# Hybrid decoder trunk: the second norm's statistics for half the tokens amid the next output tile, and one weight chunk less loaded at the head of the feed-forward's loop along k

## The chip, the cores and the metric

The kernel runs on 1 core of a Trainium2 chip (trn2). The metric is the device time of one execution in microseconds (us). The kernel before took 1461.12 us (median of 3 runs, 1460.99 to 1461.18).

The engines are named as in the profile: PE (matmul) and PEld (its weight load), DVE (VectorE), ACT (ScalarE), POOL (GpSimd) and SP, which issues most of the loads.

## The reference, cut to what matters

Two layers (DEPTH = 2) act on x, 512 tokens by 1024 features, float32:

```python
h = rmsnorm(x, norm1_w) * (1 + sc1) + sh1
u = h @ w_in                       # pool, conv, attention and gate inputs
...
x = x + g1 * (merged @ w_out)
h2 = rmsnorm(x, norm2_w) * (1 + sc2) + sh2
x = x + g2 * ((jax.nn.silu(h2 @ w_gate) * (h2 @ w_up)) @ w_down)
```

The change touches the seam between `x + g1 * (merged @ w_out)`, the second rmsnorm, and the first products `h2 @ w_gate` and `h2 @ w_up`. The rmsnorm needs, for each token, the mean of the squares of all 1024 features of the new x, so it can't be finished for a token before every output tile of that token is done.

## The kernel before, in words

**Layout.** x lies transposed in SBUF: eight tiles x0 to x7 of 128 features by 512 tokens. A product is made as three matmuls of rounded float32 parts (`mm3`, L159): high by high, high by low, low by high. So every operand, weight or activation, has a high and a low half: ACT writes the high one by a copy into the rounded type, DVE writes the low one as the difference.

**Weights.** They come in chunks of up to eight 128x128 blocks in the order in which they are used. `load_w` (L334) takes the next chunk: SP issues its load into one of three raw buffers, and `split_w` (L325) makes its two halves, `whi` on ACT and `wlo` on DVE, into one of five buffers each. A raw buffer comes free when both halves are written. `next_w(ahead)` (L351) hands out the oldest loaded chunk and first loads until more than `ahead` chunks are there, so `ahead` are left behind it; without an argument it takes `ahead_now`, which is 4 here. The `wlo` differences are pinned: DVE runs them where the program has them. While `hold[0]` is set (L329), they are also placed behind the instruction it names.

**The output product.** `tail` (L961) makes the eight output tiles n = 0 to 7 of `merged @ w_out`. Tiles 0 to 5 are made for all 512 tokens. The last two (`halved=2`) are made by halves of 256 tokens: n = 6 and 7 for the first half, then n = 6 and 7 for the second. A half tile has 8 steps along k of three matmuls, 24 matmuls. After each tile `residual` (L958, DVE) adds it into x, and `nrm.add` squares the new x and adds it to a running sum (L460 on ACT, L461 on DVE; for tile 7 the product L463 on DVE, kept apart).

**The norm.** `stat` (L465) sums the squares over the features with two matmuls against a matrix of ones, in plain float32, and `newton` (L470) makes the reciprocal root: L474 on ACT, then L475, L476 and L477 on DVE. `apply` (L481) makes one tile of h2 for a range of tokens: L485 on DVE scales, L487 on ACT gives the high half, L488 on DVE the low half, L491 on ACT a plain float32 copy for the later forms.

**The order at the seam.** When the second half of tile 6 is done, `lead()` (called at L984) takes the statistics of the first 256 tokens and applies them to h2 tiles k = 0, 1, 2, while PE makes the second half of tile 7. In the lead, `hold[0]` is set to the last L488. The feed-forward then begins with a loop along k (`HALVES + REST`, L1108): steps n = 0, 1, 2 are k = 0, 1, 2 for the first 256 tokens, steps 3, 4, 5 the same k for the other 256, then k = 3 to 7 for all 512. Each step feeds six products, three gate and three up columns, all open in PSUM until k = 7. At step n = 1, ahead of its matmuls, `second` (L521) lifts the hold, takes the statistics of the other 256 tokens and applies them to everything that is left. The weights of step k are one chunk of 384 KB, taken at the first step that uses it (L1114). For k of 4 and more `make_forms` (L1030) derives combinations of h2 tiles for a later stage. After the loop come one gate and one up column by themselves, then pairs of columns that use the forms.

**Who sets the order.** PE's order is the program's. A planner orders the other engines by its own costs, apart from the pinned instructions. Every engine works off its instructions in order.

The first norm of layer 1 passes through `tail` too, with four halved tiles (`halved=4`) and its own lead.

Of the kernel before, what the change touches and what calls it, by code (L numbers as in the profile page):

```python
# [25 lines left out]
KT = D // P  # L26
# [53 lines left out]
def hybrid_trunk(ctx, tc, xT, ws, ada, cols, pool_w, qk_w, crow, pos, con, out):  # L80
# [22 lines left out]
    def ps_mm():  # L103
        return psum.tile([P, S], F32, tag="mm", name=nm("mm"), bufs=4)

    def ps_pair():
        return psum.tile([P, 2, S], F32, tag="pair", name=nm("pair"), bufs=2)
# [23 lines left out]
    def flush_bulk():  # L131
        while bulk:
            bulk.popleft()[1]()

    def tick():
        for f in list(fibers):
            f[0] -= 1
            if f[0] <= 0:
                n = next(f[1], None)
                if n is None:  # L140
                    fibers.remove(f)
                else:
                    f[0] = n
        run_bulk(bulk_rate[0])

    def drain():
        while fibers:
            tick()

    def matmul(*a, **k):  # L150
        tc.keep_in_program_order(T.matmul(*a, **k))  # L151
# [7 lines left out]
    def mm3(o, lhs, rhs, start, stop, main=True, **more):  # L159
        matmul(o, lhs[0], rhs[0], start=start, stop=False, **more)  # L160
        matmul(o, lhs[0], rhs[1], start=False, stop=False, **more)
        matmul(o, lhs[1], rhs[0], start=False, stop=stop, **more)
        if main:
            clock[0] += o.shape[-1]
            if clock[0] >= TICK:
                clock[0] -= TICK
                tick()

    def cut(pair, *ix):
        return pair[0][ix], pair[1][ix]  # L170

    def table(func, after):

        A.activation(sm([P, 1], tag="tab", bufs=1), after, func)
# [159 lines left out]
    def load_w():  # L334
        while at[1] < min(at[0] + 1 + SUMS_AHEAD, len(items)):
            sums, sub = items[at[1]]
            if sums is not None and sub == 0:
                sums.begin()
            at[1] += 1
        sums, what = items[at[0]]  # L340
        at[0] += 1
        if sums is not None:
            return sums.load(what)
        l, blocks = what
        raw = rawt()
        fetch(raw, l, blocks)
        return split_w(raw, len(blocks))
# [3 lines left out]
    def next_w(ahead=None):  # L351
        ahead = ahead_now[0] if ahead is None else ahead
        while at[0] < len(items) and len(loaded) <= ahead:
            loaded.append(load_w())
        return loaded.popleft()

    def wblk(w, b):
        return w[0][:, b, :], w[1][:, b, :]
# [54 lines left out]
    def ada_tasks(l, parts, early=False):  # L413
        out = []
        for part in parts:
            for j in range(KT):
                out.append((1.2, lambda part=part, j=j: ada_step(l, part, j, early)))
            out.append((0.2, lambda part=part: ada_end(l, part)))
        return out
# [101 lines left out]
    def second(nrm, l, i, bank):  # L521

        hold[0] = None
        nrm.stat(BLOCK, S, bank)
        for k, lo, hi in HALVES[3:] + REST:
            nrm.apply(l, i, k, lo, hi)
# [193 lines left out]
    for l in range(L):  # L720
# [6 lines left out]
        held = {}  # L727
        for n, (k, lo, hi) in enumerate([(k, 0, S) for k in range(KT)] if l == 0 else HALVES + REST):
# [18 lines left out]
            h = norm.k(k)  # L747
# [13 lines left out]
        def feature_tile(o, w):  # L761
            for k in range(KT):
                mm3(o, wblk(w, k), norm.k(k), k == 0, k == KT - 1)
# [193 lines left out]
        def residual(k, src, lo, hi, part):  # L957
            V.scalar_tensor_tensor(x[k][:, lo:hi], src, mod[l][:, part, k:k + 1], x[k][:, lo:hi],  # L958
                                   op0=ALU.mult, op1=ALU.add)

        def tail(src_of, wblk_of, part, nk, nrm, last, lead=None, halved=2):  # L961

            for n in range(KT - halved):
                if n == KT - halved - 1:
                    flush_bulk()
                o = ps_mm()
                for k in range(nk):
                    mm3(o, wblk_of(n, k), src_of(k), k == 0, k == nk - 1)
                residual(n, o, 0, S, part)
                if nrm is not None:  # L970
                    nrm.add(n, 0, S)
                if last:
                    nc.sync.dma_start(out[n * P:(n + 1) * P, :], x[n])
            for h in range(2):
                c = slice(h * BLOCK, (h + 1) * BLOCK)
                for n in range(KT - halved, KT):
                    o = ps_mm()
                    for k in range(nk):
                        mm3(o[:, :BLOCK], wblk_of(n, k), cut(src_of(k), slice(None), c), k == 0, k == nk - 1)
                    residual(n, o[:, :BLOCK], h * BLOCK, (h + 1) * BLOCK, part)  # L980
                    if nrm is not None:
                        nrm.add(n, h * BLOCK, (h + 1) * BLOCK)
                        if h == 1 and n == KT - halved:
                            lead()  # L984
                    if last:
                        nc.sync.dma_start(out[n * P:(n + 1) * P, c], x[n][:, c])
# [12 lines left out]
        def lead(nrm, ll, i, bank):  # L999

            def go():
                nrm.stat(0, BLOCK, bank)
                for k, lo, hi in HALVES[:3]:
                    hold[0] = nrm.apply(ll, i, k, lo, hi)
            return go
# [14 lines left out]
        def glu(g, u):  # L1020
            t = tmp()
            A.activation(t, g, AF.Silu)
            V.tensor_mul(t, u, t)
            act.append(split_from(t))
# [79 lines left out]
        for part, (along, single, pairs) in enumerate(PARTS):  # L1104
            act = []
            nk = along + single + 2 * pairs
            if along:
                held = {}  # L1108
                for n, (k, lo, hi) in enumerate(HALVES + REST):
                    if n == 1:  # L1110
                        second(norm, l, 1, bank)
                        table(AF.Silu, norm.y[:, 0:1])
                    if k not in held:
                        held[k] = next_w()  # L1114
                    for z in range(2 * FA):
                        mm3(f_ps[z][:, lo:hi], wblk(held[k], z), cut(norm.k(k), slice(None), slice(lo, hi)),
                            k == 0 and lo == 0, k == KT - 1)
                    if k >= HK:
                        make_forms(k - HK)
                del held  # L1120
                for z in range(FA):
                    glu(f_ps[z], f_ps[FA + z])
            for _ in range(single):
                wg = next_w()
                g = ps_mm()
                feature_tile(g, wg)
                u = ps_mm()
                feature_tile(u, next_w())
                glu(g, u)
            bulk_rate[0] = 0.0  # L1130
            for p in range(pairs):
                glu_pair(p == pairs - 1)
            if l + 1 < L:
                if part == 0:
                    later = ada_tasks(l + 1, (SC1, SH1, SC2, SH2))
                n = DOTS[part]
                bulk.extend(later[:n])
                del later[:n]
            bulk_rate[0] = 1.5
            blk = Blocks(nk, 4)  # L1140
            if part + 1 < len(PARTS):
                for n in range(KT):
                    if n == KT // 2:
                        bulk_rate[0] = 0.0
                    o = ps_mm()
                    for k in range(nk):
                        mm3(o, blk(n, k), act[k], k == 0, k == nk - 1)
                    residual(n, o, 0, S, G2)
            elif l + 1 == L:
                tail(lambda k: act[k], blk, G2, nk, None, True)  # L1150
            else:
                flush_bulk()
                drain()
                bulk.extend(later[:5])
                del later[:5]
                bulk_rate[0], credit[0] = 0.8, 0.0
                n1 = Norm()
                table(AF.Abs_reciprocal_sqrt, f32(act[-1][1])[:, 0:1])
                scratch = ps_pair()
                bank = scratch[:, 1]  # L1160
                tail(lambda k: act[k], blk, G2, nk, n1, False, lead(n1, l + 1, 0, bank), 4)
                norm = n1
# [100 lines left out]
```

## Time and profile before

| what | value |
|---|---|
| median of 3 runs | 1461.12 us (1460.99 to 1461.18) |
| profiled execution, its own time | 1461.3 us |
| its span in the profile | 1459.5 us |
| PE busy | 1451.3 us, 99% |
| DVE busy | 1053.5 us, 72% |
| ACT busy | 665.8 us, 46% |
| POOL busy | 105.9 us, 7% |
| PE on the chain that ended last | 96% |
| matmuls | 8443 |

The timeline lists instructions in order of time: start in us from the start of the span, duration in us (of a run of equal instructions, from the first start to the last end), engine, line, operation, output and input, shapes, and the count. What stands in brackets is idle time of that engine just before and what ended it. The ends of matmuls are modelled and overlap the next start, so the distance between two starts tells what PE lost better than its idle time does. Layer 0 passes the seam at 381 to 397 us, layer 1 at 1100 to 1117 us.

### The profile page before, as it was taken

Reading aid. Unit: us, or ns where it says so; the run is one execution under the profiler, and the core shown is the slowest. Engines: PE = TensorE matmul, PEld = TensorE weight load, DVE = VectorE, ACT = ScalarE, POOL = GpSimd, SP = SyncE. Lnnn points to the kernel's source line nnn. Section 1 sums busy time; section 2 is a strip of 40 time slices with the busy share of each in tenths; the row PEclk is TensorE's granted clock in tenths of the full one; section 3 lists DMA queues with packets and bytes.
Section 4 is the critical chain, followed back from the end, with each engine's and each line's share of the span. In section 5 each row is a group of like instructions: output and inputs, shape, how many; then the busy total and the mean of one; then the engine's idle time right before and its main releaser. Section 6 shows DMA issues by size and latency. Waiting matters only on the chain.

```text
span 1459.5 us, 21946 instructions
## 1 busy us (share of the span) xinstructions
PE 1451.3 (99%) x8443; PEld 1267.9 (87%) x8443; DVE 1053.5 (72%) x1855; ACT 665.8 (46%) x1138; POOL 105.9 (7%) x157
## 2 busy tenths in 40 slices
PE   9999999999999999999999999999999999999998
PEld 7888888788989998989988878788889889989997
DVE  7988888748686867677797766776587757657663
ACT  4634555443454452535444355555335525534450
POOL 0000000001100210211000000000020102111200
PEclk9999999999999999999999999999999999999999
DMA  9645334445336766756545422222462436637522
GB/s 351 219 142 173 121 110 138 137 159 152 109 114 205 201 174 202 188 146 203 191 146 176 161 77 73 73 77 98 158 194 78 138 122 165 183 98 192 137 85 84
DMA packets 84409, 217.19 MB, mean 149 GB/s; under 512 B 10832, under 2 KB 23760, under 8 KB 84304
## 3 DMA queue, kind: packets, MB, share of 16 engines
q1 hardware_dynamic: 67456, 177.37, 35.9%
q0 software_dynamic: 16128, 37.76, 11.8%
q8 instruction: 66, 1.08, 0.3%
q10 hardware_dynamic: 720, 0.66, 0.1%
q14 instruction: 39, 0.32, 0.1%
HBM read 213.65 MB, written 2.10 MB: 148 GB/s over the span
## 4 chain that ended last, share of the span: by engine, by line
PE 96%; DVE 2%; DMA 1%; ACT 1%; issue 0%; SPq 0%; ACTq 0%
PE mm L151 82%; PE pair L151 13%; PE mm L157 2%; DVE wlo L330 1%; DMA w<-in_ada 0%; DMA x<-in_xT 0%; DVE w L376 0%; ACT whi L327 0%; DVE tmp L485 0%; DVE big L504 0%; DVE big L488 0%; ACT big L487 0%; ACT big L491 0%; DVE tmp L476 0%; DVE big L477 0%
## 5 line engine op out<-in xcount | busy, mean ns | idle before, releaser
L151 PE MATMUL mm<-big,whi 128*128 128x512 f32 (+1 forms) x4362 | 1080.9, 339 | 1.5 <-DVE big L488 0.9
L151 PEld LDWEIGHTS mm<-big,whi 128*128 128x128 f32 x4362 | 745.6, 190 | 86.6 <-DVE big L488 1.7
L151 PE MATMUL mm<-big,wlo 128*128 128x512 f32 (+1 forms) x2181 | 735.9, 337 | 0.0
L151 PEld LDWEIGHTS mm<-big,wlo 128*128 128x128 f32 x2181 | 413.8, 190 | 44.4
L327 ACT ACTIVATE whi<-raw 128x1024 fp32r<-128x1024 f32 (+2 forms) x240 | 248.9, 1039 | 288.6 <-PE mm L151 205.0
L330 DVE TENSOR_TENSOR wlo<-raw,whi 128x1024 fp32r<-128x1024 f32 (+2 forms) x240 | 283.6, 1192 | 53.1 <-ACT whi L327 52.7
L327 ACT ACTIVATE whi<-w 128x1024 fp32r<-128x1024 f32 x72 | 76.2, 1058 | 146.0 <-PE mm L151 93.1
L958 DVE SCALAR_TENSOR_TENSOR x<-mm,mod,x 128x512 f32<-128x512 f32 (+1 forms) x90 | 61.8, 688 | 82.8 <-PE mm L151 82.7
L256 POOL DMA_DIRECT2D w<-in_ws x72 | 47.7, 672 | 968.1 <-DVE w L376 390.7
L330 DVE TENSOR_TENSOR wlo<-w,whi 128x1024 fp32r<-128x1024 f32 x72 | 86.7, 1220 | 30.8 <-ACT whi L327 30.1
L376 DVE SCALAR_TENSOR_TENSOR w<-w,csil 128x1024 f32<-128x1024 f32 x80 | 95.9, 1219 | 16.3 <-DMA w<-in_ada 16.2
L151 PE MATMUL pair<-whi,big 128*128 128x512 f32 x224 | 76.7, 390 | 0.0
L258 POOL DMA_DIRECT2D w<-in_ws x72 | 64.9, 934 | 147.8 <-DMA w<-in_ws 134.4
L151 PE MATMUL pair<-big,whi 128*128 128x256 f32 (+1 forms) x376 | 74.0, 294 | 0.0
L151 PEld LDWEIGHTS pair<-big,whi 128*128 128x128 f32 x376 | 60.4, 191 | 2.2
L151 PE MATMUL mm<-whi,big 128*128 128x512 f32 x160 | 57.3, 394 | 1.5 <-ACT big L501 1.2
L151 PE MATMUL pair<-big,wlo 128*128 128x256 f32 (+1 forms) x188 | 55.3, 294 | 0.0
L918 DVE SCALAR_TENSOR_TENSOR big<-big,mm 128x512 f32<-128x512 f32 x48 | 32.6, 683 | 26.4 <-PE mm L151 26.1
L151 PEld LDWEIGHTS pair<-whi,big 128*128 128x128 f32 x224 | 42.1, 188 | 8.6
L515 DVE TENSOR_TENSOR big<-tmp,big 128x512 fp32r<-128x512 f32 x48 | 33.0, 691 | 22.3 <-ACT big L514 21.3
L514 ACT ACTIVATE big<-tmp 128x512 fp32r<-128x512 f32 x48 | 29.7, 622 | 34.6 <-DVE tmp L1097 12.5
L151 PE MATMUL pair<-wlo,big 128*128 128x512 f32 x112 | 43.6, 390 | 0.0
(192 smaller groups left out, 1242.5 us busy)
## 6 DMA issues: line engine op xcount, KB each, us to landing
raw<-in_ws SPq DMA_DIRECT2D x146, 512.0 KB, 3.5
w<-in_ada SPq DMA_DIRECT2D x80, 512.0 KB, 5.2
w<-in_ws POOLq DMA_DIRECT2D x144, 256.0 KB, 4.6
raw<-in_ws SPq DMA_DIRECT2D x64, 256.0 KB, 3.8
raw<-in_ws SPq DMA_DIRECT2D x24, 384.0 KB, 3.3
raw<-in_ada SPq DMA_DIRECT2D x16, 512.0 KB, 3.3
raw<-in_ws SPq DMA_DIRECT2D x16, 448.0 KB, 5.6
raw<-in_ws SPq DMA_DIRECT2D x36, 128.0 KB, 2.9
```

The source lines that it names most:

```text
L151: tc.keep_in_program_order(T.matmul(*a, **k))
L157: tc.keep_in_program_order(T.transpose(*a))
L256: nc.gpsimd.dma_start(dst, self.source(0, 1))
L258: nc.gpsimd.dma_start(dst, self.source(*other), accum_op=ALU.add)
L327: A.activation(hi[:, :n], raw[:, :n], AF.Copy)
L330: ins = V.tensor_sub(lo[:, :n], raw[:, :n], f32(hi)[:, :n])
L376: return V.scalar_tensor_tensor(aw, aw, 1.0, csil, op0=ALU.mult, op1=ALU.mult, accum_out=mod[l][:, part, j:j + 1])
L514: A.activation(hi, src, AF.Copy)
L515: last_split[0] = V.tensor_sub(lo, src, f32(hi))
L918: V.scalar_tensor_tensor(sg, sg, 1.0, branch, op0=ALU.add, op1=ALU.mult)
L958: V.scalar_tensor_tensor(x[k][:, lo:hi], src, mod[l][:, part, k:k + 1], x[k][:, lo:hi], op0=ALU.mult, op1=ALU.add)
```

## The change

It has two parts, both at the seam, and both act once in each layer.

The lead of the second norm is called in the middle of the second half of tile 6, behind 4 of its 8 steps along k (`nk // 2`), not at its end. The condition `halved == 2` keeps the first norm's lead, which has four halved tiles, where it was. At that point the sum of squares of the first 256 tokens needs the first halves of tiles 6 and 7, which lie ahead of it.

At step n = 0 of the feed-forward's loop, `next_w` is asked for 3 chunks ahead and not for 4. So step 0 loads k = 2 and 3 only, and k = 4 is loaded at step 1, behind `second` in the program.

```diff
                 for n in range(KT - halved, KT):
                     o = ps_mm()
                     for k in range(nk):
+
+                        if nrm is not None and halved == 2 and (h, n, k) == (1, KT - halved, nk // 2):
+                            lead()
                         mm3(o[:, :BLOCK], wblk_of(n, k), cut(src_of(k), slice(None), c), k == 0, k == nk - 1)
                     residual(n, o[:, :BLOCK], h * BLOCK, (h + 1) * BLOCK, part)
                     if nrm is not None:
                         nrm.add(n, h * BLOCK, (h + 1) * BLOCK)
-                        if h == 1 and n == KT - halved:
+                        if h == 1 and n == KT - halved and halved != 2:
                             lead()
...
                     if k not in held:
-                        held[k] = next_w()
+                        held[k] = next_w(3 if n == 0 else None)
```

In the order of instructions that results, these are the differences, the same in both layers. PE: the two statistics matmuls stand behind 12 of the 24 matmuls of the tile. ACT: the root L474 comes ahead of the split of chunk k = 3, and that split ahead of the first L487; the square of tile 6 (L460) comes behind the first L487, the split of k = 4 behind the second L487, the split of k = 7 behind all of `second` and the first split of the forms. DVE: L475 to L477 come ahead of the residual of tile 6's second half, which comes ahead of the three L485; then L488, L461, L488, the residual and the square of tile 7 (L958, L463), L488, and the low halves of k = 2 and 3. The low half of k = 4 comes behind the last L488 of `second`, ahead of k = 5 and 6; that of k = 7 behind the first of the forms. SP and, at the seam, POOL issue the same loads in the same order.

## The prediction

> **What bounds the kernel now.** I read the page first, then PE's waits, then the timeline where they lie.
>
> ```profile
> span 1459.5 us, 21946 instructions
> PE 1451.3 (99%) x8443; PEld 1267.9 (87%) x8443; DVE 1053.5 (72%) x1855; ACT 665.8 (46%) x1138; POOL 105.9 (7%) x157
> ...
> PE mm L151 <- DVE big L488: 0.9, 4, 0.3
> PE mm L151 <- ACT big L487: 0.4, 2, 0.2
> ```
>
> PE bounds the kernel: 1451.3 us of a span of 1459.5 are busy. Of its few waits (us in total, times, longest), six are for `apply` of a norm, L487 and L488: three per layer. PE's own timeline of the seam in layer 0 tells more than these totals:
>
> ```profile
> 380.94 0.40 PE L151 MATMUL mm<-big,whi 128*128 128x256 f32 x2
> ...
> 382.38 0.40 PE L151 MATMUL mm<-big,whi 128*128 128x256 f32 x2
> ...
> 383.82 1.02 PE L151 MATMUL pair<-big,ones 128*128 128x256 f32 x4
> 384.50 0.59 PE L151 MATMUL mm<-big,whi 128*128 128x256 f32 x2
> 384.92 0.28 PE L151 MATMUL mm<-big,wlo 128*128 128x256 f32 x1
> ...
> 387.43 0.28 PE L151 MATMUL mm<-big,wlo 128*128 128x256 f32 x1
> 387.91 0.39 PE L151 MATMUL mm<-big,whi 128*128 128x256 f32 x1 [0.20 <-ACT big L487]
> 388.56 0.39 PE L151 MATMUL mm<-big,whi 128*128 128x256 f32 x1 [0.26 <-DVE big L488]
> 388.78 0.28 PE L151 MATMUL mm<-big,wlo 128*128 128x256 f32 x1
> ...
> 390.69 1.02 PE L151 MATMUL pair<-big,ones 128*128 128x256 f32 x4
> ...
> 395.86 0.28 PE L151 MATMUL mm<-big,whi 128*128 128x256 f32 x1
> ...
> 396.55 0.28 PE L151 MATMUL mm<-big,wlo 128*128 128x256 f32 x1
> ```
>
> Tile 6's second half starts at 380.94, its middle is 382.38, its end 383.82: 24 matmuls, 0.12 us from start to start. The statistics take 383.82 to 384.50. The last matmul of tile 7 starts at 387.43, so the first three of the feed-forward should start at 387.55, 387.67 and 387.79. The third starts at 388.78: **stall 1 costs 0.99 us**, first for the high half of h2 tile 0, then for the low one. At 395.86 the second 256 tokens of k = 0 begin; the third matmul should start at 396.10 and starts at 396.55: **stall 2 costs 0.45 us**. That is 1.44 us in this layer.
>
> The waits total only 0.9 + 0.4 = 1.3 us over both layers, because modelled ends cover part of each gap; the starts give 1.44 for one. Layer 1 passes the seam alike, 719.7 us later:
>
> ```profile
> 380.00:398.00 18.00, 17.35 (x135) 16.53 (x134) 13.68 (x29) 9.60 (x20) 0.00 (x0) 1.00 0.20 67
> 1099.70:1117.70 18.00, 17.34 (x135) 16.53 (x134) 13.69 (x29) 9.61 (x20) 0.00 (x0) 1.00 0.21 66
> ```
>
> (Busy us and counts of PE, PEld, DVE, ACT and POOL, then PE's granted clock, DMA's share, GB/s.) The same counts and times, clock 1.00. So at most 2 x 1.44 = 2.88 us are to be had at these two seams.
>
> [...]
>
> **The change, part by part.** It adds and removes no instruction. *The lead* issues its two statistics matmuls 1.44 us earlier (382.38 for 383.82). PE's own time for them stays 0.68 us, and the two steps behind them take 0.42 (384.50 to 384.92) for 0.24. This is paid once wherever they stand, so I take 0; the far bound is a second seam, 0.18 per layer. A bound below nothing has no reason: the tile isn't shortened.
>
> The lead's chain on DVE and ACT, in layer 0:
>
> ```profile
> 381.66 0.42 DVE L463 TENSOR_TENSOR big<-x 128x256 f32<-128x256 f32 x1
> ...
> 383.90 0.84 ACT L327 ACTIVATE whi<-raw 128x768 fp32r<-128x768 f32 x1 [4.64 <-PE mm L151]
> ...
> 384.96 0.46 ACT L474 ACTIVATE tmp<-pair,epst 128x256 f32<-128x256 f32 x1
> ...
> 385.45 0.42 DVE L475 SCALAR_TENSOR_TENSOR tmp<-pair,tmp 128x256 f32<-128x256 f32 x1
> ...
> 386.37 0.43 DVE L477 SCALAR_TENSOR_TENSOR big<-tmp,tmp 128x256 f32<-128x256 f32 x1
> ...
> 386.83 1.27 DVE L485 SCALAR_TENSOR_TENSOR tmp<-x,am,big 128x256 f32<-128x256 f32 x3
> ...
> 387.35 0.51 ACT L487 ACTIVATE big<-tmp,mod 128x256 fp32r<-128x256 f32 x1 [1.93 <-DVE tmp L485]
> ...
> 388.02 0.48 DVE L488 SCALAR_TENSOR_TENSOR big<-tmp,mod,big 128x256 fp32r<-128x256 f32 x1
> ```
>
> *The wait that the move adds.* PE now asks for the square of tile 7 (L463) at 382.38; it ends at 381.66 + 0.42 = 382.08, so 0.30 us are spare. Behind that wait would stand 12 matmuls of tile 6, tile 7 and all else on PE.
>
> *Stall 1.* The root moves from 384.96 to 383.52, L475 from 385.45 to 384.01, L477 from 386.37 to 384.93. DVE then runs the residual of tile 6 first, which costs the chain 0.5 (L958 to L463, 388.42 to 388.93, in the next fence): L485 at 385.85 for 386.83. ACT's split of k = 3 waits for the end of tile 6, now 384.50, and ends by 385.5, ahead of L487 at 385.85 + 0.52 = 386.37. Its high half serves PE 0.56 later (387.35 to 387.91), at 386.93; PE asks at 387.55. L488 follows L487 by 0.67: 387.04. The matmul on the low half starts 0.54 after L488 (388.02 to 388.56), at 387.58; PE asks at 387.67. Stall 1 goes, with 0.1 us spare.
>
> *Stall 2.* These rows carry the second half's chain:
>
> ```profile
> 388.42 0.47 DVE L958 SCALAR_TENSOR_TENSOR x<-mm,mod,x 128x256 f32<-128x256 f32 x1
> 388.93 0.42 DVE L463 TENSOR_TENSOR big<-x 128x256 f32<-128x256 f32 x1
> ...
> 390.22 0.48 DVE L488 SCALAR_TENSOR_TENSOR big<-tmp,mod,big 128x256 fp32r<-128x256 f32 x1 [0.32 <-ACT big L487]
> 390.63 2.69 DVE L330 TENSOR_TENSOR wlo<-raw,whi 128x768 fp32r<-128x768 f32 x3
> 393.23 0.42 DVE L475 SCALAR_TENSOR_TENSOR tmp<-pair,tmp 128x256 f32<-128x256 f32 x1
> ...
> 395.80 0.48 DVE L488 SCALAR_TENSOR_TENSOR big<-tmp,mod,big 128x256 fp32r<-128x256 f32 x1
> ...
> 391.82 0.47 ACT L474 ACTIVATE tmp<-pair,epst 128x256 f32<-128x256 f32 x1 [1.23 <-PE pair L151]
> ```
>
> From the first L488 to the third took 388.02 to 390.22, 2.20 us. It now holds L461 as well (0.3 to 0.4), so the third L488 starts at 387.04 + 2.20 + 0.36 = 389.6 at the latest. L463 of tile 7 stands just ahead of it and ends by 389.5; PE asks for it behind k = 0, at 387.55 + 18 x 0.12 = 389.71. No wait, 0.2 spare.
>
> The splits held three low halves in 393.23 - 390.63 = 2.60, 0.87 each. Now two: L475 at 389.6 + 0.41 + 1.74 = 391.75, 1.48 earlier. ACT's root, 1.13 behind the statistics (390.69 to 391.82), is at 390.84 and no limit. L488 of k = 0 moves from 395.80 to 394.32, and the low matmul could start at 394.86. PE asks 5.17 behind the start of the statistics (390.69 to 395.86) at 394.88, and for the low half at 395.00. Stall 2 goes, with 0.14 spare. With three splits it would have been 395.73, a stall of 0.7: the second edit is worth that.
>
> *Price of the second edit.* The low half of k = 4 now waits behind all of `second`:
>
> ```profile
> 407.35 0.39 PE L151 MATMUL mm<-big,wlo 128*128 128x512 f32 x1
> ...
> 404.65 0.71 ACT L487 ACTIVATE big<-tmp,mod 128x512 fp32r<-128x512 f32 x1
> ...
> 405.39 0.75 DVE L488 SCALAR_TENSOR_TENSOR big<-tmp,mod,big 128x512 fp32r<-128x512 f32 x1 [1.21 <-ACT big L487]
> 406.07 2.69 DVE L330 TENSOR_TENSOR wlo<-raw,whi 128x768 fp32r<-128x768 f32 x3
> ...
> 412.95 1.06 ACT L327 ACTIVATE whi<-raw 128x1024 fp32r<-128x1024 f32 x1 [1.11 <-DMA raw<-in_ws]
> ...
> raw<-in_ws SPq DMA_DIRECT2D x24, 384.0 KB, 3.3
> ...
> 423.38 10.88 PE mm L151 x48
> ```
>
> PE first needs it at 407.35, which becomes 405.91. The last L488 (405.39) waits for ACT's L487; both move 1.48 earlier, and about 0.7 more if ACT's split of k = 7 really falls behind. So the low half starts at 403.9 to 404.6 and ends 0.95 later, at 404.9 to 405.6: 0.3 to 1.0 spare. Cost nothing.
>
> *The queues.* On SP the load of k = 7 waits for the raw buffer of k = 4, freed now at about 405 instead of 393.2. It lands 3.3 us later (median row), near 409; PE needs it three steps behind k = 4, each 18 matmuls of 0.227 (10.88 / 48), at 405.5 + 12.3 = 417.8. The loads behind it may land up to 3.3 later than 412.95; the lone columns that use them start at 423.38, less 1.44. ACT and DVE may halt a microsecond on k = 7's split ahead of the forms, which are first used after those columns, at 423.38 + 10.88 - 1.44 = 432.8. POOL's order is unchanged here. I cost these at nothing; if the cover were gone, the price is 3.3 us per layer at most.
>
> **Sum.** Per layer 0.99 + 0.45 = 1.44 goes. The spares of 0.1 and 0.14 are no larger than my reading errors, so I keep back 0.09: 1.35, in two layers 2.7 us. Against its own time the profiled execution goes from 1461.3 to 1458.6; it stands 0.2 above the median, which goes from 1461.12 to **1458.4**.
>
> **The rivals.**
>
> *One stall stays.* If the low halves or L463 come 0.5 us later than worked out, stall 2 stays or a stall of its size takes its place: 1461.12 - 2 x 0.99 = 1459.1. For it speaks that all spares are thin; against it, that each row above was put late. 0.18.
>
> *The statistics stop the tile.* If L463 reached PE later than 382.38, PE would lose the delay in the middle of tile 6. A matmul on a fresh DVE result started 0.54 after that instruction's start (L488): 381.66 + 0.54 = 382.20, so I see none. With a seam of 0.18 and 0.3 of waiting per layer: 1458.4 + 1.0 = 1459.4. 0.05. [...]
>
> *Slower: k = 4's low half is late.* If it comes behind the other two of the run at 406.07, or as late as that through ACT, it ends at 408.76 and PE waits 408.76 - 405.91 = 2.85 per layer: 1461.12 + 2 x (2.85 - 1.44) = 1463.9. It decides from an end later than 405.91 + 1.44 = 407.35, 1.8 us beyond my latest. 0.07.
>
> *It does nothing.* The gain is handed back before the pairs, where DVE and the loads lag: 1461.1. Against it: PE shows no wait there now. 0.06.
>
> **How the numbers follow.** My forecast has 0.64. What a measurement of this kernel can tell from no change is about 0.2%, 2.9 us, and the most that I can find is 2.88: so nearly all of the forecast, and the three milder cases, count as the same. Faster by over 0.2% needs the whole 2.88 and a little that I don't see: 0.07. Slower by over 0.2% needs the third rival at its full price or past it: 0.06. The rest, 0.87, is within. The forecast's own range is 1458.1 to 1459.0; taken to one stall staying and the stopped tile, with half a stall on top, it is 1458.0 to 1460.2, which leaves out 0.13.
>
> **What would show it.** PE's starts between tile 7 and k = 0 should step by 0.12, and so again at the second half; the four L488 and two L487 should be gone from its waits. The statistics should start 1.44 before tile 6 ends, L475 of the second half 0.9 behind the root. The forecast is wrong if PE waits at `pair<-big,ones`, at a low half of k = 4, or at the forms.

## The result, and the profile after

The kernel after takes 1458.89 us (median of 21 runs, 1458.56 to 1460.02). Beside it the kernel before took 1460.94 (21 runs, 1460.66 to 1463.23). The ratio is 0.9986, 95% interval 0.9980 to 0.9992: faster by 2.05 us, a gain of less than 0.2%, which the interval still sets apart from no change. The forecast was 1458.4, with 1458.0 to 1460.2 around it. The profiled execution took 1458.56 us, 0.33 below the median.

The page of the kernel after, its span and engines:

```profile
span 1456.8 us, 21945 instructions
PE 1449.7 (100%) x8443; PEld 1267.1 (87%) x8443; DVE 1053.3 (72%) x1855; ACT 665.5 (46%) x1138; POOL 105.9 (7%) x157
```

And its waits, all rows for PE (us in total, times, longest):

```profile
PE pair L151 <- POOL ones L199: 1.1, 1, 1.1
PE mm L151 <- ACT big L501: 1.1, 1, 1.1
PE pair L151 <- DVE big L692: 0.5, 2, 0.3
PE mm L151 <- DVE w L635: 0.2, 1, 0.2
PE mm L151 <- DVE big L504: 0.2, 1, 0.2
```

The six waits on L487 and L488 are gone. PE's timeline of the seam in layer 0, kernel after (it runs here some 0.3 us earlier than before):

```profile
380.62 0.40 PE L151 MATMUL mm<-big,whi 128*128 128x256 f32 x2
...
382.06 1.02 PE L151 MATMUL pair<-big,ones 128*128 128x256 f32 x4
382.74 0.58 PE L151 MATMUL mm<-big,whi 128*128 128x256 f32 x2
...
387.11 0.28 PE L151 MATMUL mm<-big,wlo 128*128 128x256 f32 x1
387.23 0.40 PE L151 MATMUL mm<-big,whi 128*128 128x256 f32 x2
387.47 0.28 PE L151 MATMUL mm<-big,wlo 128*128 128x256 f32 x1
...
388.19 0.28 PE L151 MATMUL mm<-big,wlo 128*128 128x256 f32 x1
388.44 0.50 PE L151 MATMUL mm<-big,whi 128*128 128x256 f32 x2
388.78 0.28 PE L151 MATMUL mm<-big,wlo 128*128 128x256 f32 x1
...
389.61 1.03 PE L151 MATMUL pair<-big,ones 128*128 128x256 f32 x4
...
394.79 0.40 PE L151 MATMUL mm<-big,whi 128*128 128x256 f32 x2
395.03 0.28 PE L151 MATMUL mm<-big,wlo 128*128 128x256 f32 x1
```

The statistics start 382.06 - 380.62 = 1.44 into the tile and take 0.68 as before. Tile 7's last matmul (387.11) and the first of k = 0 (387.23) are 0.12 apart, the third stands at 387.47: stall 1 is gone. At 394.79 and 395.03 the second half steps by 0.12 too: stall 2 is gone. But one step is new: from 388.19 to 388.44 it is 0.25 and to 388.78 two steps take 0.34, so 0.59 for what should be 0.36. **0.23 us go there** (0.236 unrounded), at the fourth product of k = 0. DVE in the same stretch:

```profile
381.34 0.42 DVE L463 TENSOR_TENSOR big<-x 128x256 f32<-128x256 f32 x1
...
386.53 0.47 DVE L488 SCALAR_TENSOR_TENSOR big<-tmp,mod,big 128x256 fp32r<-128x256 f32 x1
386.93 0.42 DVE L461 TENSOR_TENSOR big<-big,tmp 128x256 f32<-128x256 f32 x1
387.51 0.48 DVE L488 SCALAR_TENSOR_TENSOR big<-tmp,mod,big 128x256 fp32r<-128x256 f32 x1 [0.16 <-ACT big L487]
387.91 0.48 DVE L958 SCALAR_TENSOR_TENSOR x<-mm,mod,x 128x256 f32<-128x256 f32 x1
...
391.18 0.42 DVE L475 SCALAR_TENSOR_TENSOR tmp<-pair,tmp 128x256 f32<-128x256 f32 x1
...
393.76 0.48 DVE L488 SCALAR_TENSOR_TENSOR big<-tmp,mod,big 128x256 fp32r<-128x256 f32 x1
```

`ps_mm` hands out four PSUM banks (into which PE writes its products) in turn, so the fourth bank of the feed-forward's first step is the one in which tile 7's second half was made. It is free when L958 has added that half into x, at 387.91 + 0.48 = 388.39, and PE takes it 0.05 later. Before, L958 ended at 388.89 against a fourth product held back by stall 1; now the stall is gone, and two L488 and L461 stand ahead of L958.

To see all of PE's gains and losses, the starts of the 8443 matmuls, which apart from the statistics come in the same order in all kernels, were set side by side. Kernel after against before, us:

| place | layer 0 | layer 1 |
|---|---|---|
| statistics amid tile 6 | 0.00 | 0.00 |
| tile 7 to k = 0 (stall 1) | -0.99 | -0.99 |
| fourth product of k = 0 (bank) | +0.23 | +0.23 |
| second half of k = 0 (stall 2) | -0.45 | -0.44 |
| seam, with rounding | -1.20 | -1.20 |
| third part of the feed-forward, near 504 us | +0.28 | 0.00 |

The sum is -2.40 + 0.28 = -2.12, against the 2.05 of the medians. Elsewhere the two executions differ at the first 55 us (-0.3) and at 842 us (-0.3). Another execution of the same kernel (`after_again`) shows 0.0 and +0.1 at those two places, so the kernel's order alone does not set them. At 842 us DVE stood idle ahead of L376 for a late load, 0.6 us in the kernel before and 0.7 in `after_again`, but not in the profiled execution of the kernel after. Whole spans therefore say less here than the starts at the seams.

### The profile page after: what moved, and what is told of

The parts are those of the page before. It is cut to its first block, busy times and chain, and to the rows that moved or that the text cites. A ratio compares the mean times of both kernels' runs of the same rounds, so it can differ in the third digit from the quotient of the medians.

```text
span 1456.8 us, 21945 instructions
## 1 busy us (share of the span) xinstructions
PE 1449.7 (100%) x8443; PEld 1267.1 (87%) x8443; DVE 1053.3 (72%) x1855; ACT 665.5 (46%) x1138; POOL 105.9 (7%) x157
## 4 chain that ended last, share of the span: by engine, by line
PE 96%; DMA 2%; DVE 1%; ACT 0%; issue 0%; SPq 0%; POOL 0%
PE mm L151 82%; PE pair L151 13%; PE mm L157 2%; DMA w<-in_ws 1%; DMA w<-in_ada 0%; DMA x<-in_xT 0%; DVE w L376 0%; DVE wlo L330 0%; ACT whi L327 0%; DVE big L504 0%; SPq L190 0%; DVE tmp L497 0%; ACT big L501 0%; DVE w L635 0%; DVE big L702 0%
## 5 line engine op out<-in xcount | busy, mean ns | idle before, releaser
L327 ACT ACTIVATE whi<-raw 128x1024 fp32r<-128x1024 f32 (+2 forms) x240 | 248.8, 1039 | 277.8 <-PE mm L151 193.7
L330 DVE TENSOR_TENSOR wlo<-raw,whi 128x1024 fp32r<-128x1024 f32 (+2 forms) x240 | 283.8, 1192 | 53.7 <-ACT whi L327 53.4
L327 ACT ACTIVATE whi<-w 128x1024 fp32r<-128x1024 f32 x72 | 76.2, 1058 | 149.1 <-PE mm L151 88.7
L958 DVE SCALAR_TENSOR_TENSOR x<-mm,mod,x 128x512 f32<-128x512 f32 (+1 forms) x90 | 61.8, 688 | 79.6 <-PE mm L151 79.5
L330 DVE TENSOR_TENSOR wlo<-w,whi 128x1024 fp32r<-128x1024 f32 x72 | 86.7, 1220 | 32.0 <-ACT whi L327 31.4
L376 DVE SCALAR_TENSOR_TENSOR w<-w,csil 128x1024 f32<-128x1024 f32 x80 | 95.8, 1219 | 14.0 <-DMA w<-in_ada 13.8
```

The lines of the kernel that those rows point to most:

```text
L327: A.activation(hi[:, :n], raw[:, :n], AF.Copy)
L330: ins = V.tensor_sub(lo[:, :n], raw[:, :n], f32(hi)[:, :n])
L376: return V.scalar_tensor_tensor(aw, aw, 1.0, csil, op0=ALU.mult, op1=ALU.mult, accum_out=mod[l][:, part, j:j + 1])
```

## The experiments

All are compared with the kernel before, run beside them on the same chip: 1461.12 us for the first eight, 1461.01 for the last three.

### The changed kernel again

No edit.

> The changed kernel once more, for a second profile. Against the one before, its first profile gains 1.20 us at each seam, 0.33 in the first 55 us and 0.30 near 842 us, and loses 0.23 near 504 us, where a weight sum lands late. If these last three are chance of the single execution, they differ here, while the two seams stand at 1.20 each; if the loss near 504 us is what the gain uncovers, it is here again. Time 1458.9.

Measured: 1459.27 us (1458.53 to 1460.37), ratio 0.9986 (0.9978 to 0.9995). Both seams -1.19, bank wait +0.24, near 504 us +0.30. The gains at the seams and the new wait near 504 us are there again: they belong to the kernel. The time is 0.4 above the 1458.9 that was expected, and 0.24 above what the starts add up to.

### Each part alone

`lead_alone` undoes the second part, `ahead_alone` the first:

```diff
-                        held[k] = next_w(3 if n == 0 else None)
+                        held[k] = next_w()
```

> The lead stands in the middle of tile 6, and step 0 still loads up to four chunks ahead. My theory: stall 1 goes (0.99 us per layer, two layers) and the low halves of k = 2, 3 and 4 stand ahead of the second half's root chain, so L475 there comes 0.87 us later than in the changed kernel (near 392.05) and PE waits 0.25 to 0.45 us at the second 256 tokens of k = 0. Time 1459.2, some 0.5 to 0.8 above the changed kernel. Rival, the lead does it all: no wait there, the time of the changed kernel, 1458.9.

> Step 0 loads three chunks ahead, and the lead stands at the end of tile 6 as before. My theory: stall 1 stays whole (0.99 us per layer), stall 2 (0.45 us) goes, since the root chain of the second half starts 0.87 us earlier on DVE: 1460.94 - 0.9 = 1460.0. Rival, the edit pays only with the lead: 1460.9.

Measured: `lead_alone` 1459.80 us (1459.27 to 1460.60), ratio 0.9992 (0.9983 to 1.0000); `ahead_alone` 1460.14 (1459.78 to 1461.51), ratio 0.9994 (0.9985 to 1.0003). Against before, per layer: `lead_alone` -0.99 at stall 1, +0.23 at the bank, -0.11 at stall 2, and the +0.29 near 504 us; `ahead_alone` -0.45 at stall 2 and nothing else. So each part removes the stall it was credited with, and the bank wait and the loss near 504 us come with the lead. The profiled execution of `lead_alone` also lost 0.26 once, near 1178 us, where no other execution does. Its time is 0.6 above the 1459.2 that was expected; the wait itself, 0.34 per layer, is within the 0.25 to 0.45. The timeline of `lead_alone`, PE and then DVE, shows what is left of stall 2:

```profile
395.70 0.75 PE L151 MATMUL mm<-big,whi 128*128 128x256 f32 x2
396.28 0.28 PE L151 MATMUL mm<-big,wlo 128*128 128x256 f32 x1
...
395.52 0.48 DVE L488 SCALAR_TENSOR_TENSOR big<-tmp,mod,big 128x256 fp32r<-128x256 f32 x1
```

The third matmul starts 0.58 after the first for 0.24: 0.34 lost. The low half serves PE at 395.52 + 0.54 = 396.06, 0.24 after PE asks; the step behind a wait is 0.22 for 0.12, as in the kernel before (388.56 to 388.78), which makes 0.34.

### Tile 7's bank used last

```diff
-        f_ps = [ps_mm(), ps_mm(), ps_mm(), ps_mm(), pair_a[:, 0], pair_a[:, 1]]
+        f_ps = [ps_mm(), ps_mm(), ps_mm(), pair_a[:, 0], pair_a[:, 1], ps_mm()]
```

> The changed kernel, and of the six PSUM banks of the loop along k the one that held tile 7 serves the last product of a step, not the fourth. In the changed kernel PE loses 0.24 us per layer at the fourth product of the first step (start 388.44), which the old one did not. Theory: that product takes tile 7's bank and waits for tile 7's residual, which now stands behind two L488 and L461 on DVE; six matmuls later (0.72 us) the bank is free, so the loss goes: 0.47 us less than the changed kernel, 1458.4. Rival, the loss is no wait for the bank: it stays at the fourth product or moves with the step, and the time stays 1458.9.

Measured: 1458.53 us (1458.09 to 1459.40), ratio 0.9983 (0.9974 to 0.9992). PE's timeline around the fourth product, and DVE's residual:

```profile
389.10 0.28 PE L151 MATMUL mm<-big,wlo 128*128 128x256 f32 x1
389.22 0.40 PE L151 MATMUL pair<-big,whi 128*128 128x256 f32 x2
...
388.82 0.48 DVE L958 SCALAR_TENSOR_TENSOR x<-mm,mod,x 128x256 f32<-128x256 f32 x1
```

L958 stands where it stood against PE, and PE steps over it by 0.12: its product goes to another bank. The seam is -1.43 in both layers, the whole of both stalls. The bank wait is shown.

### The lead earlier and later in the tile

```diff
-  if nrm is not None and halved == 2 and (h, n, k) == (1, KT - halved, nk // 2):
+  if nrm is not None and halved == 2 and (h, n, k) == (1, KT - halved, nk // 4):
```

and `3 * nk // 4` for the later one. (A half tile has 8 steps of three matmuls, so the quarter lies behind step 2, not 3 of 12 as the expectation has it; in time it is the same.)

> Edit against the changed kernel: the lead's work is handed out at a quarter of output tile 6's second 256 tokens (contraction step 3 of 12) instead of the middle. The lead's first instruction for TensorE is the statistics matmul, which needs VectorE's L463 square. In the changed kernel's trace that square starts at 381.34, and statistics asked for at 382.06 did not wait; a quarter handed out earlier is asked for at about 381.3, and TensorE's products elsewhere start about 0.54 us after the VectorE instruction that they follow. Theory (statistics are bound by the square, and TensorE runs its queue in order): TensorE stops about 0.5 us per layer amid tile 6, the wait on tile 7's bank at the fourth product of step k=0 (0.24 per layer) stays or shrinks little, and the time is 1459.4 to 1459.9. Rival (nothing holds the statistics there): as the changed kernel, 1458.9.

> Edit against the changed kernel: the lead's work is handed out at three quarters of output tile 6's second 256 tokens (contraction step 9 of 12), about 0.72 us of TensorE work later. Theory (the chain from the statistics to the first low half L488 is serial and had only about 0.3 us to spare at step k=0): the first low half comes about 0.7 later and TensorE waits 0.3 to 0.5 us per layer at the start of step k=0; the second 256 tokens of k=0 wait 0.2 to 0.6 too, unless the first wait covers it; 1459.5 to 1460.5. Rival (the middle has slack to spare, the point matters little): 1458.9.

Measured: the quarter 1458.71 us (1458.19 to 1459.00), ratio 0.9982 (0.9972 to 0.9992); three quarters 1459.59 (1459.31 to 1460.79), ratio 0.9990 (0.9981 to 0.9999). The expectation for the quarter missed. The statistics in its timeline:

```profile
382.15 1.18 PE L151 MATMUL pair<-big,ones 128*128 128x256 f32 x4
```

They take 1.18 for 1.02: PE loses 0.15 per layer, not 0.5. Only the second statistics matmul reads the square of L463, which starts at 382.16; the first reads the running sum, which was ready (its last L461 ended at 379.79 + 0.42 = 380.21), and covers most of the wait. In return the chain starts earlier: L475 stands 2.50 behind the start of the tile for 3.07, and tile 7's residual L958 6.96 behind it for 7.29. So L958 ends at 388.88, ahead of the fourth product at 389.27, and the bank wait is gone: the seam is -1.28, better than the middle's -1.20. Nor does the +0.28 near 504 us appear.

At three quarters the expectation held, but for a first wait slightly over its 0.3 to 0.5. PE's timeline, and the low half it waits for:

```profile
387.75 0.29 PE L151 MATMUL mm<-big,whi 128*128 128x256 f32 x1
388.30 0.39 PE L151 MATMUL mm<-big,whi 128*128 128x256 f32 x1 [0.26 <-DVE big L488]
...
387.77 0.48 DVE L488 SCALAR_TENSOR_TENSOR big<-tmp,mod,big 128x256 fp32r<-128x256 f32 x1
```

The low half serves PE 0.53 after its start, and PE loses 0.53 per layer (0.43, and 0.10 in the step behind). The seam is -0.91. So at the middle the first half's chain has a little to spare, and 0.72 later it hasn't.

### Two chunks ahead

```diff
-                        held[k] = next_w(3 if n == 0 else None)
+                        held[k] = next_w(2 if n == 0 else None)
```

> Edit against the changed kernel: two chunks ahead in the step that opens the feed-forward's loop along k, not three; so k=3's low half too is computed behind the second 256 tokens' statistics on VectorE. In the changed kernel's trace k=4's low half, which stands there, ended at 404.24; k=3's first product starts at about 401.7. Theory (the low half behind the second statistics is held by VectorE's order, as the forecast's slower rival has it for k=4): TensorE waits about 2 to 3 us per layer for k=3's low half, 1463 to 1465. Rival (VectorE has room to bring it earlier): within 0.3 of the changed kernel, 1458.9.

Measured: 1463.30 us (1463.08 to 1464.20), ratio 1.0016 (1.0006 to 1.0027): slower than before. The row of its waits, and its timeline:

```profile
PE mm L151 <- DVE wlo L330: 3.4, 2, 1.7
```

```profile
401.50 0.63 PE L151 MATMUL mm<-big,whi 128*128 128x512 f32 x2
403.80 0.50 PE L151 MATMUL mm<-big,wlo 128*128 128x512 f32 x1 [1.66 <-DVE wlo L330]
...
402.79 2.69 DVE L330 TENSOR_TENSOR wlo<-raw,whi 128x768 fp32r<-128x768 f32 x3
```

The low half of k = 3 now stands behind the second L488 run, ends some 0.95 after 402.79, and PE waits: +1.95 and +2.03 by the starts. This is the mechanism of the forecast's slower rival, one chunk further on. DVE didn't run the pinned split earlier than the program has it: ahead of the last L488 (402.12) it stood idle for 0.47, waiting for ACT's L487, though the high half that the split needs was there, as PE read it from 401.50 on.

### The loss near 504 us

The timelines of the kernel after there, ACT, DVE and PE:

```profile
501.63 1.06 ACT L327 ACTIVATE whi<-w 128x1024 fp32r<-128x1024 f32 x1 [0.31 <-DMA w<-in_ws]
...
502.73 1.23 DVE L330 TENSOR_TENSOR wlo<-w,whi 128x1024 fp32r<-128x1024 f32 x1 [0.35 <-ACT whi L327]
503.87 0.41 DVE L1089 TENSOR_TENSOR tmp<-tmp,mm 128x256 f32<-128x256 f32 x1
...
504.34 0.50 PE L151 MATMUL mm<-big,whi 128*128 128x256 f32 x2
```

ACT's split comes 0.28 later against PE than in the kernel before; the pinned DVE split behind it is late, then L1089, and PE waits for that. The profile names a load as what ended ACT's idle time. But the idle time is the same, 0.31 to 0.32, in every execution with this loss, while loads vary. Counting ACT's recorded instructions from the first, semaphore waits included, gives this:

| kernel | number of that split | it starts after the end of its semaphore wait, us | PE's step at the loss, us |
|---|---|---|---|
| before, `ahead_alone` | 577 | 0.045 | 0.12 |
| `lead_quarter` | 576 | 0.042 | 0.12 |
| after, `lead_alone`, `bank_last`, `lead_threequarter` | 575 | 0.322 | 0.35 |
| `after_again`, `ahead_two` | 575 | 0.336 | 0.36 |

The lead's move leaves two semaphore waits fewer ahead of it on ACT. Numbers that leave 63 when divided by 128 (63, 191, ... 575, 703, ...) were slow in other places as well: in the nine executions above and the first of `act_pad` together, behind a semaphore wait and from 60 us on, 32 of 39 such activations start 0.32 to 0.34 after the wait's end, and 42 of the 3765 others. So `act_pad` adds two tiny copies to `bank_last`, in ACT's first microseconds:

```diff
+    pad = const.tile([P, 2], F32, name="pad")
+    for j in range(2):
+        A.activation(pad[:, j:j + 1], blank, AF.Copy)
```

> Edit against the kernel with tile 7's bank used last: two one-element copies on ScalarE in its first microseconds, where it waits for loads. The lead's move left ScalarE's stream two semaphore instructions shorter, and in all four kernels with the move ScalarE's split L327 of a weight near 502 us starts 0.3 us later against TensorE, and TensorE waits 0.23 us at its third feed-forward part. Theory A (the place of the instruction in ScalarE's stream decides it): with two instructions more ahead of it the 0.23 us is gone, and the time is 1458.3. Theory B (something else in the schedule): the 0.23 stays, 1458.5.

Measured: 1458.67 us (1458.27 to 1459.34), ratio 0.9984 (0.9975 to 0.9993). The split is number 576 now (one semaphore wait fell away). Its timeline, ACT and DVE, where three added lines make L327 and L330 into L330 and L333:

```profile
501.34 0.63 ACT L1100 ACTIVATE tmp<-tmp 128x512 f32<-128x512 f32 x1 [2.38 <-DVE tmp L1088]
502.00 1.06 ACT L330 ACTIVATE whi<-w 128x1024 fp32r<-128x1024 f32 x1
...
503.10 1.22 DVE L333 TENSOR_TENSOR wlo<-w,whi 128x1024 fp32r<-128x1024 f32 x1
```

The split starts 0.042 after its wait, DVE has no idle time ahead of its part, and PE's step is 0.12: the loss near 504 us is gone. In exchange number 703, now an activation behind a wait, starts 0.324 late, at a place where PE doesn't need it. So theory A holds for the wait; the time didn't fall as it said. This execution lost 0.24 near 1340 us, where ACT waited for a load:

```profile
1341.20 1.07 ACT L330 ACTIVATE whi<-raw 128x1024 fp32r<-128x1024 f32 x1 [1.78 <-DMA raw<-in_ws]
```

Three kernels were run once more beside each other:

> The kernel with tile 7's bank used last and the two one-element copies, again, beside the same without the copies and the changed kernel on one chip. If 0.28 us of the wait near 502 us is gone in every execution, and the late load that cost 0.24 near 1340 us in its first profile was chance: 0.25 to 0.3 below the kernel without the copies, about 1458.25, and that late load is not there. If the late load belongs to the kernel: 1458.5, and it is there again.

> Tile 7's bank used last, without the copies: 1458.5 by the starts of the matmuls (2 x 1.44 gone, 0.28 come).

> The changed kernel: 1459.0 by the starts of the matmuls (2 x 1.20 gone, 0.28 come).

Measured: `act_pad_2` 1458.53 us (1458.27 to 1460.07), `bank_last_2` 1458.43 (1458.27 to 1459.53), `after_3` 1458.79 (1458.57 to 1459.22), each with ratio 0.9984 (0.9975 to 0.9993). The wait near 504 us is gone again with the copies, and the late load near 1340 us is not there: that was chance. Yet the time with the copies is no lower. What they cost elsewhere stays open: both executions with the copies lost nearly 0.6 us in the first 55 us against the kernel before, but so did one of the two without (+0.61 and -0.16). Tile 7's bank used last is 0.36 and 0.74 below the kernel after by the medians of its two comparisons, 0.47 by the starts; the ratios' intervals overlap, so the gain rests on the starts alone. No version has a lower median; `lead_quarter` equals it by the starts (-2.55 for -2.57 in all).

## Why the prediction was right, and where it was off

**The sums.** Median of before beside it, plus the seams and the place near 504 us by the starts, against what was measured:

| kernel | seams | near 504 us | sum | measured |
|---|---|---|---|---|
| after | -2.40 | +0.28 | 1458.82 | 1458.89 |
| `lead_alone` | -1.71 | +0.29 | 1459.70 | 1459.80 |
| `ahead_alone` | -0.89 | 0 | 1460.23 | 1460.14 |
| `bank_last` | -2.86 | +0.29 | 1458.55 | 1458.53 |
| `lead_quarter` | -2.55 | 0 | 1458.57 | 1458.71 |
| `lead_threequarter` | -1.81 | +0.28 | 1459.59 | 1459.59 |
| `ahead_two`, with +3.98 at k = 3 | -2.39 | +0.31 | 1463.02 | 1463.30 |
| `act_pad` | -2.86 | 0 | 1458.26 | 1458.67 |

All but the last agree to 0.3 us or better. Of the repeats, `after_again` (1459.03 for 1459.27), `after_3` (1458.89 for 1458.79) and `bank_last_2` (1458.44 for 1458.43) do so too; `act_pad_2` (1458.15 for 1458.53) is off by 0.4 like `act_pad`. So these few places explain the change, but not what the copies cost.

**Both stalls.** Right, in place and in size: 0.99 and 0.45 per layer, read from starts, went whole. By idle time (1.3 us in both layers) the forecast would have been 1459.8; the measured gain of 2.05 is beyond that. So here the starts told what was left, and the idle time less than half of it (1.3 of 2.88).

**The spares.** The first low half was given 0.1 us. The low half L488 serves PE at 386.53 + 0.54 = 387.07, PE asks at 387.35: 0.28. The term that was too large is tile 6's residual, put at 0.5: from L477 to L485 the chain takes 0.74 (384.61 to 385.35) where it took 0.46, so the residual costs 0.28. The second half was given 0.14 and has 394.91 - (393.76 + 0.54) = 0.61, 0.24 of it because the bank wait delays PE. That the second edit is worth 0.7 beside the lead was too much: it is worth 0.34. In `lead_alone` the chain ended 0.26 earlier than it was put, and the bank wait made PE ask 0.23 later, which leaves 0.24, and 0.10 in the step behind. Alone the edit is worth 0.45.

**The statistics.** Asked for at 382.06, 0.72 after L463 started (381.34), no wait, and no second seam: right. `lead_quarter` shows that even 0.7 earlier costs 0.15 only.

**What is late next: missed.** The forecast left out that the residual of tile 7 also frees a PSUM bank, which PE writes at the fourth product. That is 0.236 per layer, 0.47 in all. The step that failed is the one that followed tile 7's residual and square to the statistics alone, "No wait, 0.2 spare": the square is in time, and the residual ahead of it, behind two L488 and L461, is not, for another reader.

**What stood outside the seam: missed.** +0.28 near 504 us, through ACT's count of instructions. The step is "It adds and removes no instruction": that holds for the work, but ACT has two semaphore waits fewer ahead of that split, and the forecast took the places behind the seam as unchanged.

With these two the forecast's 2.88 becomes 2.88 - 0.47 - 0.28 = 2.13. The 0.09 per layer that were kept back for reading errors covered a quarter of it. The gain is 0.67 short of the forecast (2.05 for 2.72). The time is only 0.5 above it, since the kernel before measured 0.18 lower beside it than the 1461.12 from which the forecast starts. That it fell inside the forecast's own range of 1458.1 to 1459.0 is in part luck: of the two later measurements 1458.79 lies inside and 1459.27 outside.

**The root.** The forecast had "L475 of the second half 0.9 behind the root". In the kernel after it is 0.50 (390.68 to 391.18). ACT's row and DVE's low halves ahead of L475:

```profile
390.68 0.48 ACT L474 ACTIVATE tmp<-pair,epst 128x256 f32<-128x256 f32 x1 [1.27 <-PE pair L151]
...
389.44 1.82 DVE L330 TENSOR_TENSOR wlo<-raw,whi 128x768 fp32r<-128x768 f32 x2
```

That is the distance which L475 has when DVE is waiting for the root (383.18 to 383.69 in the lead). But the two low halves, 0.87 each, are done at the same moment, 389.44 + 1.74 = 391.18, and DVE has no idle time there: the two chains end together. The bank wait stands ahead of the statistics on PE and so delays the root. In `bank_last`, without that wait, ACT and DVE show this:

```profile
391.36 0.47 ACT L474 ACTIVATE tmp<-pair,epst 128x256 f32<-128x256 f32 x1 [1.04 <-PE pair L151]
...
392.09 0.42 DVE L475 SCALAR_TENSOR_TENSOR tmp<-pair,tmp 128x256 f32<-128x256 f32 x1
```

The distance is 0.73, and the low halves set the second half, as the forecast has it. Of the 0.4 by which the 0.9 was off, 0.23 is the bank wait, which the forecast left out.

**The rivals.** The slower one did not come: the last L488 run let the low half of k = 4 start at 403.29 and PE asked at 405.83.

```profile
403.29 2.69 DVE L330 TENSOR_TENSOR wlo<-raw,whi 128x768 fp32r<-128x768 f32 x3
...
405.38 0.62 PE L151 MATMUL mm<-big,whi 128*128 128x512 f32 x2
405.83 0.39 PE L151 MATMUL mm<-big,wlo 128*128 128x512 f32 x1
```

It was the first of the three, done by about 404.24, with 1.6 us to spare where 0.3 to 1.0 were given. `ahead_two` shows that the rival's mechanism is real and what it costs, 2.0 us per layer. No queue cost anything that the starts show: the loads behind the seam had their slack. "The statistics stop the tile" did not come. "One stall stays" did not come either, as both stalls went whole; but its 1459.1 is nearer to the measured 1458.89 than the forecast's 1458.4, and a smaller stall did take the place of the old ones: 0.24 per layer, for a bank that no rival named.

## What to carry to other kernels

When a stall is taken away, list for each engine's new order not only what it writes but what it frees: here a PSUM bank that was reused in the shadow of the old stall became the next wait, 0.236 us per layer, and another order of reuse took it away with no loss at the seam (-1.43 in `bank_last` for -1.20). Read a stall from the starts of the matmuls on both sides of it, and compare kernels start by start: single executions of one kernel differ by 1.5 to 2.6 us here (the 21 runs each of after and before), and the whole change is worth 2.05.

## What the runs showed of the hardware that was not expected

Activations at every 128th place of ACT's stream started some 0.28 us late when a semaphore wait stood just ahead of them: 0.32 behind the wait's end for 0.04, in 32 of the 39 cases counted above. In a run of activations no such delay is seen: in the kernel after, numbers 447, 959 and 1087 start 0.09 to 0.12 ahead of the end of the activation before them, as others in a run do (median 0.09). The page of the kernel after lists, among its DMA queues (packets, MB, share of 16 engines' span):

```profile
q14 instruction: 39, 0.32, 0.1%
```

ACT did not wait for such a packet to arrive. In the kernel after its split stood from 501.31 to 501.63, and from 501 to 502 us these queues alone had packets:

```profile
q1 hardware_dynamic: 66, 0.27, 66.9%
q0 software_dynamic: 48, 0.07, 40.3%
```

In all 13 profiled executions together, an instruction packet was under way in 1 of 42 such late starts, and the next one began 0.6 us or more behind each. What costs the 0.28 us stays open.

At four places a TensorE wait cost some 0.10 us more than its delay: the step behind it took 0.22 for 0.12, in stall 1, in `lead_alone`, in `lead_threequarter` and at the bank in the kernel after alike.
